# Token sums pinned in one head, seven-product units moved apart, and low parts made by ScalarE and an adding DMA in a hybrid decoder layer

## The chip, the cores and the metric

One core of a Trainium2 chip runs one launch of the kernel. The metric is the device time of that launch in microseconds, the median over several runs. A second figure beside it is the span of one profiled execution, from the first to the last instruction.

## The reference

The layer has 256 tokens, a model width of 2048 and one input matrix that feeds two token mixers side by side. Cut to what matters here:

```python
h = rmsnorm(x, pre_norm_g)
q_a, c_kv, k_rope, z_mla, c_in, b_gate, c_gate, z_conv, g_mla, g_conv = split(h @ w_in)
y_mla  = (causal_mla_attention(q_a, c_kv, k_rope) * silu(z_mla)) @ w_o_mla
y_conv = (b_gate * short_conv(c_gate * c_in) * silu(z_conv)) @ w_o_conv
merged = sigmoid(g_mla) * y_mla + sigmoid(g_conv) * y_conv
return x + rmsnorm(merged @ w_out, post_norm_g)
```

Everything is float32. The change concerns `g_mla` and `g_conv`, two products of the 256 x 2048 normalised input with 2048 x 2048 matrices, which the kernel calls the gate blocks, and some preparation for them during the attention heads.

## The kernel before, in words

**Precision.** TensorE multiplies in a rounded float32 form (`F32R`). Each operand is therefore split into a high part (the rounded value) and a low part (the rest). A product a*b is three matmuls: high*high, high*low, low*high (`product`, L252). The split of a weight is `split_act` (L267): ScalarE copies the raw weight into the rounded tile (L268), and VectorE subtracts that from the raw weight (L269).

**Units.** All weights come as a list of units, `plan`, each 128 x 2048 numbers, 1 MB, in the order in which TensorE uses them. SyncE issues a unit's load into one of three `raw` buffers (`load_raw`, L154, the DMA at L161). `split_unit` (L170) makes the parts, in one of three `whi` and one of three `wlo` buffers (`slot`, L166). `take(i)` (L237) is called when TensorE's matmuls of unit i are written down. In the gate blocks it first asks for the splits up to unit i+2 and the loads up to unit i+3 (L239). With three slots, unit i+2 uses the slot of unit i-1, so its split can start when the matmuls of unit i-1 are done, and it has the time of units i and i+1.

**Order.** Matmuls, and whatever goes through `keep_in_program_order`, keep the order of the program on their engine. All other instructions are placed by a planner that runs a timing model when the kernel is built: among instructions of an engine that it takes to be ready, the earlier in the program goes first. On the chip each engine then runs its list strictly in order. The DMAs on GpSimd's queue that turn tiles around (L355, L359) and that bring shifted rows for the short convolution (L753) are pinned; so are the convolution's additions on VectorE (L769).

**Heads.** Sixteen heads, `for h in range(H)`, each with four units of one channel product (`channels(h, 0..3)`, tiles `cv`), and between them the scores (`sc`), the softmax, the turning of the probabilities (`pt`) and the values (`o`). In odd heads up to 13 one more unit, ahead of the last channel unit, makes the next heads' queries and keys (`qn`, `kn`). After the heads come four gate blocks (matrix n, half b), then the products `sq` with `w_o_mla` and `w_o_conv`, then `out`.

**Gate blocks.** `gate_block` (L936) works on 1024 output columns and has eight units. Five are plain ("whole"): two 128-row slices of the weight, four outputs (two token tiles by two column halves), so 2 x 4 products or 24 matmuls. Three are pairs: two slices k and k+4 that are combined as in Strassen's scheme (Winograd's form), seven products in place of eight, so 21 matmuls. For a pair, `split_pair` (L204) first forms sums and differences of the four raw quarters on VectorE (`tf` and one quarter of `raw`, three instructions at L212), then splits `raw` into `whi`, `wlo` and `tf` into `thi`, `tlo`. There is one `tf`, one `thi` and one `tlo` buffer. The other side of the pairs is the same for all blocks: `token_sums` (L782) forms sums of token tiles (`xf`, L790 to L795) and splits them into `xs`; VectorE does all of it but four copies by ScalarE. It is called once, in head 13, ahead of that head's last channel unit, and its instructions are not pinned.

After the last pair of a block (L968) the products 1, 5, 6 and 7 are joined: ScalarE copies products 1 and 5 from PSUM (L971, L972), VectorE forms `u` in three instructions (L974 to L976). At the block's end VectorE adds these to the four outputs (L980) and ScalarE takes the sigmoid (L981).

The order of a block's units is made by `gate_kinds` (L1105): pair, plain, pair, plain, pair, plain, plain, plain; in the first block the last two plain ones stand in front.

Of the kernel before, what the change touches and what calls it, by code (L numbers as in the profile page):

```python
# [12 lines left out]
F32R = mybir.dt.float32r  # L13
I32 = mybir.dt.int32
AF = mybir.ActivationFunctionType
ALU = mybir.AluOpType
PSUM = bass.MemoryType.PSUM

P = 128
# [3 lines left out]
KD = D // P  # L23
H = 16
# [60 lines left out]
def tile_layer(ctx: ExitStack, tc: tile.TileContext, xw, x, pos, pvec, post_g, wc, wz, wcv, wkr, wqk, wqr, wv, cwr, wsq, wg, out):  # L85
# [84 lines left out]
    def split_unit(i):  # L170
        t, (_, w, kind) = raws.pop(i), plan[i]
        if i == u_kr:
            t = t[:, :w].rearrange("p (k c) -> p k c", k=KD)
            both, parts = slot(i, False)[0], []
            for h in range(2):
                part = both[:, h * HALF : (h + 1) * HALF].rearrange("p (k j c) -> p k j c", k=KD // 2, j=2)
                split_act(part[:, :, 0], part[:, :, 1], t[:, h * KD // 2 : (h + 1) * KD // 2])
                parts.append(part.rearrange("p k j c -> p k (j c)"))
            splits[i] = parts
            return  # L180
        if i <= u_qa[-1]:

            hi, lo = slot(i)
            for j in range(2):
                k, o = 2 * i + j, j * XW
                src = x_first if k == 0 else t[:, o : o + S]
                split_scaled(x_both, src, k)
                split_act(hi[:, j * R : (j + 1) * R], lo[:, j * R : (j + 1) * R], t[:, o + S : o + XW], True)
            splits[i] = hi, lo
            return  # L190
        if u_out[3, 0] <= i < u_out[3, 3]:
            hi, lo = (op.tile([P, UNIT], F32R, name=f"w{o}{i}") for o in ("hi", "lo"))
        else:
            hi, lo = slot(i)
        if kind == "pair":
            splits[i] = split_pair(i, t, hi, lo)
            return
        n = HALF if kind == "half" else UNIT
        for h in range(0, w, n):
            e = min(h + n, w)  # L200
            split_act(hi[:, h:e], lo[:, h:e], t[:, h:e])
        splits[i] = hi, lo
# [64 lines left out]
    def split_act(hi, lo, src, keep=False):  # L267
        a = nc.scalar.activation(hi, src, AF.Copy)  # L268
        b = nc.vector.tensor_tensor(lo, src, hi.bitcast(F32), op=ALU.subtract)  # L269
        if keep:  # L270

            tc.keep_in_program_order(a)
            tc.keep_in_program_order(b)
# [508 lines left out]
    def token_sums(pool):  # L782


        both = x_both[:, :, :].bitcast(F32).rearrange("p (g k) c -> p g k c", k=STEP)[:, :2, :PAIRS]
        xs = pool.tile([P, 4, PAIRS, 2, P], F32R, name="xs")
        xf = pool.tile([P, 2, PAIRS, S], F32, name="xf", tag="tf", bufs=1)
        tt = nc.vector.tensor_tensor
        for g in range(2):
            tt(xf[:, g], both[:, g, :, :S], both[:, g, :, S:], op=ALU.add)  # L790
        (a11, a21), (a12, a22) = [[xf[:, g, :, t * P : (t + 1) * P] for t in range(NT)] for g in range(2)]
        tt(a22, a21, a22, op=ALU.add)
        tt(a21, a11, a21, op=ALU.subtract)
        tt(a11, a22, a11, op=ALU.subtract)
        tt(a12, a12, a11, op=ALU.subtract)  # L795
        for i, f in enumerate((a22, a11, a21, a12)):
            split_act(xs[:, i, :, 0], xs[:, i, :, 1], f)
        return xs

    cv_w = bp.tile([P, NT, 512], F32, name="cv_w")  # L800
    tap, coming, ps_by_head = None, [], {}
# [7 lines left out]

    dstack = main.enter_context(ExitStack())  # L810

    for h in range(H):
        v, at = divmod(h, HV)

# [35 lines left out]
        else:  # L850
            pt = turn(ps_by_head.pop(h - 1))
        channels(h, 1)
        if at == 0:
            arrive()
            coming.append(gates_turn(v, 1))
        else:
            values(h - 1, pt)
# [7 lines left out]
        if at and h < H - 1:  # L865
            arrive()
        channels(h, 2)
        if at == 0:
            arrive()
            if v:  # L870
                coming.append(channels_join(v - 1, 0))
# [6 lines left out]
        if h == H - 3:  # L878
            lstack.close()
            d0 = dstack.enter_context(tc.tile_pool(name="d0", bufs=1))  # L880
            xs = token_sums(d0)
        channels(h, 3)
        if at == 0:
            while coming:
                arrive()
# [45 lines left out]
    def wide(name):  # L931
        return d1.tile([P, 512], F32, name=name, tag=name, bufs=1)
# [3 lines left out]
    def gate_block(n, b, last):  # L936
# [6 lines left out]
        for i, (kind, _) in enumerate(kinds):  # L943
            for m in TAGS if kind == "pair" else ():
                ends[m] = i
            for m in (2, 3, 4, 0) if kind == "whole" else ():
                ends[m] = i
        last_pair = max(i for i, (kind, _) in enumerate(kinds) if kind == "pair")

# [4 lines left out]
        for i, (kind, ks) in enumerate(kinds):  # L954
            if last:
                for v in {6: (0, 1), 7: (2,)}.get(i, ()):
                    split_branch(v)
            w = take(units[i])
            if kind == "pair":
                for m in TAGS:  # L960
                    if m:
                        add_to(m, side(m, ks[0]), w[m], i, True)
            else:
                for m, t, half in ((2, 0, 0), (3, 0, 1), (4, 1, 0), (0, 1, 1)):
                    for j, k in enumerate(ks):
                        a = [x_both[:, k, o + t * P : o + (t + 1) * P] for o in (0, S)]
                        add_to(m, a, w(2 * j + half, 512), i, j == len(ks) - 1)
            if i == last_pair:  # L968
                p1, p5 = wide("p1"), wide("p5")
                u = d1.tile([P, 3, 512], F32, name="u", tag="u", bufs=1)  # L970
                nc.scalar.activation(p1[:, :], ps[1][:, :], AF.Copy)  # L971
                nc.scalar.activation(p5[:, :], ps[5][:, :], AF.Copy)  # L972
                tt = nc.vector.tensor_tensor
                tt(u[:, 0], ps[6][:, :], p1[:, :], op=ALU.add)  # L974
                tt(u[:, 2], ps[7][:, :], u[:, 0], op=ALU.add)
                tt(u[:, :2], u[:, 0::2], p5[:, :].rearrange("p (o c) -> p o c", o=1).to_broadcast([P, 2, 512]), op=ALU.subtract)  # L976
        for m, t, half, other in ((2, 0, 0, p1[:, :]), (3, 0, 1, u[:, 0]), (4, 1, 0, u[:, 2]), (0, 1, 1, u[:, 1])):
            o = 1024 * b + 512 * half
            g = sg[:, n, t, o : o + 512]
# [125 lines left out]
def gate_kinds():  # L1105

    pairs = [("pair", (k, k + STEP)) for k in range(PAIRS)]
    paired = {k for _, ks in pairs for k in ks}
    rest = [k for k in range(KD) if k not in paired]
    plain = [("whole", ks) for ks in zip(rest[::2], rest[1::2])]  # L1110
    alternate = []
    for i, pair in enumerate(pairs):
        alternate += [pair, plain[i]]
    alternate += plain[PAIRS:]
    late = plain[-2:] + [u for u in alternate if u not in plain[-2:]]
    return {(n, b): late if n == b == 0 else alternate for n in range(2) for b in range(2)}


def _cols(w):
# [99 lines left out]
```

## Time and profile before

| | |
|---|---|
| median of 3 runs | 1051.96 us (1051.76 to 1052.58) |
| the profiled execution, its own time | 1052.53 us |
| its span | 1050.7 us |
| TensorE matmul busy | 1026.5 us, 98% |
| VectorE busy | 743.0 us, 71% |
| ScalarE busy | 532.5 us, 51% |
| GpSimd busy | 180.7 us, 17% |
| mean granted TensorE clock | 0.991 |
| DMA | 231.00 MB, mean 220 GB/s |

The profile's page gives each engine's busy time, the chain of work that ended last, and groups of instructions with the idle time in front of them and what ended it. A row `PE sc L90 <- DVE kn L269: 5.8, 1, 5.8` of the waits reads: TensorE's matmuls into `sc`, issued at line 90, waited for VectorE's instruction on `kn` at line 269, 5.8 us in total, once, 5.8 us the longest. A row of the timeline has start, length, engine, line, operation, output and inputs with their shapes, the count, and in brackets the idle time of the engine before it and what ended that. A row of the windows table has, for a stretch of time, the busy time of TensorE, its weight loads, VectorE, ScalarE and GpSimd, each with the number of instructions, then the granted TensorE clock, the DMA engines' busy share and GB/s.

### The profile page before, as it was taken

What the parts mean: (1) busy time and instruction counts of PE and PEld (TensorE: products, weight loads), DVE (VectorE), ACT (ScalarE), POOL (GpSimd) and SP (SyncE); (2) the same over time, 40 slices, a digit from 0 to 9 for tenths busy, and PEclk for the clock granted to TensorE, in tenths of its full rate; (3) what the DMA queues carried; (4) which work ended last, traced back from release to release, by engine and by line L of the source; (5) the groups of instructions that cost most, each with busy time, mean ns of one, the idle gap of its engine ahead of it and who ended that gap; (6) DMA issues with size and microseconds to landing.
All of it is one profiled execution on the core that took longest, in us unless ns stands there. A gap on an engine that the chain in (4) does not pass through costs nothing.

```text
span 1050.7 us, 12467 instructions
## 1 busy us (share of the span) xinstructions
PE 1026.5 (98%) x4658; PEld 852.6 (81%) x4658; DVE 743.0 (71%) x960; ACT 532.5 (51%) x675; POOL 180.7 (17%) x345
## 2 busy tenths in 40 slices
PE   9999999999999999999998999899999999999997
PEld 7887888888888888888886878688888888888885
DVE  7578759677687767777776799788885545666562
ACT  7766546455555455564553545555564433333451
POOL 7621220204212142112312220000000000232000
PEclk9999999999999999999998999899999999999998
DMA  8754765668666685765765765455555555677842
GB/s 337 295 199 177 257 212 212 226 214 275 197 243 195 226 284 199 244 216 203 264 231 196 248 216 186 165 194 202 200 206 195 199 200 192 220 252 247 330 160 80
DMA packets 41948, 231.00 MB, mean 220 GB/s; under 512 B 7520, under 2 KB 8224, under 8 KB 18976
## 3 DMA queue, kind: packets, MB, share of 16 engines
q1 hardware_dynamic: 29808, 197.54, 52.8%
q0 software_dynamic: 11648, 29.38, 9.1%
q10 hardware_dynamic: 432, 3.29, 0.8%
q8 instruction: 36, 0.59, 0.2%
q14 instruction: 24, 0.20, 0.0%
HBM read 214.48 MB, written 11.53 MB: 215 GB/s over the span
## 4 chain that ended last, share of the span: by engine, by line
PE 83%; DVE 9%; issue 4%; ACT 2%; DMA 1%; SPq 0%; DVEq 0%; ACTq 0%
PE cv L90 28%; PE sq L90 17%; PE g L90 10%; PE z L90 8%; PE out L90 8%; DVE wlo L269 4%; PE qn L90 2%; PE ckv L90 2%; ACT whi L268 2%; PE kn L90 2%; PE qa L90 2%; PE vv L90 2%; PE sc L90 1%; PE o L90 1%; DVE tlo L269 1%
## 5 line engine op out<-in xcount | busy, mean ns | idle before, releaser
L269 DVE TENSOR_TENSOR wlo<-raw,whi 128x1024 fp32r<-128x1024 f32 (+2 forms) x290 | 423.5, 1485 | 229.0 <-ACT whi L268 228.4
L268 ACT ACTIVATE whi<-raw 128x1024 fp32r<-128x1024 f32 (+2 forms) x292 | 357.3, 1259 | 373.8 <-PE sq L90 96.9
L90 PE MATMUL cv<-whi,x_both 128*128 128x512 f32 x1024 | 324.1, 391 | 2.7 <-DVE cv_w L736 2.7
L90 PEld LDWEIGHTS cv<-whi,x_both 128*128 128x128 f32 x1024 | 192.9, 188 | 43.1 <-DVE cv_w L736 3.7
L90 PE MATMUL cv<-wlo,x_both 128*128 128x512 f32 x512 | 200.2, 391 | 0.0
L90 PE MATMUL g<-whi,x_both 128*128 128x512 f32 x368 | 119.8, 390 | 0.0
L90 PEld LDWEIGHTS cv<-wlo,x_both 128*128 128x128 f32 x512 | 96.4, 188 | 18.8
L90 PEld LDWEIGHTS g<-whi,x_both 128*128 128x128 f32 x368 | 69.5, 189 | 14.6
L90 PE MATMUL z<-whi,x_both 128*128 128x512 f32 x256 | 80.6, 390 | 0.0
L90 PE MATMUL sq<-whi,x_both 128*128 128x512 f32 x256 | 79.0, 389 | 0.0
L90 PE MATMUL sq<-whi,cv_both 128*128 128x512 f32 x256 | 79.0, 389 | 0.0
L90 PE MATMUL out<-whi,x_both 128*128 128x512 f32 x256 | 79.0, 389 | 0.0
L355 POOL DMA_DIRECT2D far<-via x64 | 35.3, 559 | 225.8 <-DVE via L348 224.8
L90 PE MATMUL g<-wlo,x_both 128*128 128x512 f32 x184 | 71.8, 390 | 0.0
L355 POOL DMA_DIRECT2D far<-sg x32 | 17.5, 552 | 311.5 <-DVE sg L1025 270.2
L90 PEld LDWEIGHTS sq<-whi,x_both 128*128 128x128 f32 x256 | 48.0, 188 | 10.0
L90 PEld LDWEIGHTS sq<-whi,cv_both 128*128 128x128 f32 x256 | 48.0, 188 | 9.9
L90 PEld LDWEIGHTS out<-whi,x_both 128*128 128x128 f32 x256 | 48.0, 188 | 9.9
L90 PEld LDWEIGHTS z<-whi,x_both 128*128 128x128 f32 x256 | 48.1, 188 | 9.9
L90 PE MATMUL z<-wlo,x_both 128*128 128x512 f32 x128 | 49.8, 389 | 0.0
L90 PE MATMUL sq<-wlo,x_both 128*128 128x512 f32 x128 | 49.8, 389 | 0.0
L90 PE MATMUL sq<-wlo,cv_both 128*128 128x512 f32 x128 | 49.8, 389 | 0.0
(242 smaller groups left out, 1327.6 us busy)
## 6 DMA issues: line engine op xcount, KB each, us to landing
raw<-wcv_dram SPq DMA_DIRECT2D x64, 1024.0 KB, 5.4
raw<-wsq_dram SPq DMA_DIRECT2D x48, 1024.0 KB, 4.8
raw<-wg_dram SPq DMA_DIRECT2D x32, 1024.0 KB, 4.7
raw<-wz_dram SPq DMA_DIRECT2D x16, 1024.0 KB, 4.8
raw<-wqk_dram SPq DMA_DIRECT2D x8, 1024.0 KB, 6.7
cw<-cwr_dram POOLq DMA_DIRECT2D x24, 256.0 KB, 6.3
raw<-wc_dram SPq DMA_DIRECT2D x4, 1024.0 KB, 10.0
raw<-wv_dram SPq DMA_DIRECT2D x4, 1024.0 KB, 5.3
```

The source lines that it names most:

```text
L90: return tc.keep_in_program_order(nc.tensor.matmul(*a, **kw))
L268: a = nc.scalar.activation(hi, src, AF.Copy)
L269: b = nc.vector.tensor_tensor(lo, src, hi.bitcast(F32), op=ALU.subtract)
L355: tc.keep_in_program_order(nc.gpsimd.dma_start(out=f[i], in_=m))
```

## The change

**Token sums.** `token_sums` becomes a generator. Its tiles are still made in head 13; its instructions are now pinned on VectorE and (the four copies) ScalarE, and stand in head 14 in three places: the two additions of high and low parts after channel unit 1, four sums and differences after unit 2, the four splits after unit 3.

**Order of the units.** The pairs stand at places 0, 3 and 5 of a block (1, 3 and 5 in the first), so two other units lie between the first and the second, one between the second and the third, and two between the third and the next block's first.

**Added units.** The plain units at places 2 and 6 of each block, eight in all, are of a new kind. ScalarE writes the negative rounded weight into `wlo`; a DMA on GpSimd's queue adds the raw weight to it, read once more from DRAM; ScalarE then makes `whi`. VectorE has no part in it. These DMAs are not pinned. They are 1 MB each.

**Joining.** Product 5 is no longer copied by ScalarE; the last step of `u` is two VectorE instructions that read it in PSUM, in place of one.

```diff
--- before.py
+++ after.py
@@ -194,6 +194,12 @@
             hi, lo = slot(i)
         if kind == "pair":
             splits[i] = split_pair(i, t, hi, lo)
+            return
+        if kind == "added":
+            nc.scalar.activation(lo[:, :], t[:, :], AF.Copy, scale=-1.0)
+            nc.gpsimd.dma_start(out=lo[:, :], in_=plan[i][0].bitcast(F32R), accum_op=ALU.add)
+            nc.scalar.activation(hi[:, :], t[:, :], AF.Copy)
+            splits[i] = hi, lo
             return
         n = HALF if kind == "half" else UNIT
         for h in range(0, w, n):
@@ -785,17 +791,25 @@
         both = x_both[:, :, :].bitcast(F32).rearrange("p (g k) c -> p g k c", k=STEP)[:, :2, :PAIRS]
         xs = pool.tile([P, 4, PAIRS, 2, P], F32R, name="xs")
         xf = pool.tile([P, 2, PAIRS, S], F32, name="xf", tag="tf", bufs=1)
-        tt = nc.vector.tensor_tensor
+
+        def tt(*a, op):
+            tc.keep_in_program_order(nc.vector.tensor_tensor(*a, op=op))
+
+        yield xs
         for g in range(2):
             tt(xf[:, g], both[:, g, :, :S], both[:, g, :, S:], op=ALU.add)
+            yield
         (a11, a21), (a12, a22) = [[xf[:, g, :, t * P : (t + 1) * P] for t in range(NT)] for g in range(2)]
         tt(a22, a21, a22, op=ALU.add)
         tt(a21, a11, a21, op=ALU.subtract)
+        yield
         tt(a11, a22, a11, op=ALU.subtract)
         tt(a12, a12, a11, op=ALU.subtract)
+        yield
         for i, f in enumerate((a22, a11, a21, a12)):
-            split_act(xs[:, i, :, 0], xs[:, i, :, 1], f)
-        return xs
+            split_act(xs[:, i, :, 0], xs[:, i, :, 1], f, True)
+            if i % 2:
+                yield
 
     cv_w = bp.tile([P, NT, 512], F32, name="cv_w")
     tap, coming, ps_by_head = None, [], {}
@@ -809,6 +823,7 @@
 
     dstack = main.enter_context(ExitStack())
 
+    sums = None
     for h in range(H):
         v, at = divmod(h, HV)
 
@@ -850,6 +865,9 @@
         else:
             pt = turn(ps_by_head.pop(h - 1))
         channels(h, 1)
+        if h == H - 2:
+            next(sums)
+            next(sums)
         if at == 0:
             arrive()
             coming.append(gates_turn(v, 1))
@@ -865,6 +883,9 @@
         if at and h < H - 1:
             arrive()
         channels(h, 2)
+        if h == H - 2:
+            next(sums)
+            next(sums)
         if at == 0:
             arrive()
             if v:
@@ -878,8 +899,12 @@
         if h == H - 3:
             lstack.close()
             d0 = dstack.enter_context(tc.tile_pool(name="d0", bufs=1))
-            xs = token_sums(d0)
+            sums = token_sums(d0)
+            xs = next(sums)
         channels(h, 3)
+        if h == H - 2:
+            next(sums)
+            next(sums)
         if at == 0:
             while coming:
                 arrive()
@@ -943,7 +968,7 @@
         for i, (kind, _) in enumerate(kinds):
             for m in TAGS if kind == "pair" else ():
                 ends[m] = i
-            for m in (2, 3, 4, 0) if kind == "whole" else ():
+            for m in (2, 3, 4, 0) if kind != "pair" else ():
                 ends[m] = i
         last_pair = max(i for i, (kind, _) in enumerate(kinds) if kind == "pair")
 
@@ -966,14 +991,14 @@
                         a = [x_both[:, k, o + t * P : o + (t + 1) * P] for o in (0, S)]
                         add_to(m, a, w(2 * j + half, 512), i, j == len(ks) - 1)
             if i == last_pair:
-                p1, p5 = wide("p1"), wide("p5")
+                p1 = wide("p1")
                 u = d1.tile([P, 3, 512], F32, name="u", tag="u", bufs=1)
                 nc.scalar.activation(p1[:, :], ps[1][:, :], AF.Copy)
-                nc.scalar.activation(p5[:, :], ps[5][:, :], AF.Copy)
                 tt = nc.vector.tensor_tensor
                 tt(u[:, 0], ps[6][:, :], p1[:, :], op=ALU.add)
                 tt(u[:, 2], ps[7][:, :], u[:, 0], op=ALU.add)
-                tt(u[:, :2], u[:, 0::2], p5[:, :].rearrange("p (o c) -> p o c", o=1).to_broadcast([P, 2, 512]), op=ALU.subtract)
+                for o in (1, 0):
+                    tt(u[:, o], u[:, 2 * o], ps[5][:, :], op=ALU.subtract)
         for m, t, half, other in ((2, 0, 0, p1[:, :]), (3, 0, 1, u[:, 0]), (4, 1, 0, u[:, 2]), (0, 1, 1, u[:, 1])):
             o = 1024 * b + 512 * half
             g = sg[:, n, t, o : o + 512]
@@ -1107,13 +1132,15 @@
     pairs = [("pair", (k, k + STEP)) for k in range(PAIRS)]
     paired = {k for _, ks in pairs for k in ks}
     rest = [k for k in range(KD) if k not in paired]
-    plain = [("whole", ks) for ks in zip(rest[::2], rest[1::2])]
-    alternate = []
-    for i, pair in enumerate(pairs):
-        alternate += [pair, plain[i]]
-    alternate += plain[PAIRS:]
-    late = plain[-2:] + [u for u in alternate if u not in plain[-2:]]
-    return {(n, b): late if n == b == 0 else alternate for n in range(2) for b in range(2)}
+    plain = list(zip(rest[::2], rest[1::2]))
+    kinds = {}
+    for block in range(4):
+        at = (0, 3, 5) if block else (1, 3, 5)
+        left, units = iter(plain), []
+        for i in range(KD // 2):
+            units.append(pairs[at.index(i)] if i in at else ("added" if i in (2, 6) else "whole", next(left)))
+        kinds[divmod(block, 2)] = units
+    return kinds
 
 
 def _cols(w):
```

## Prediction

> **What bounds the kernel now.** I read the page first, then TensorE's waits, then a table of windows over the heads and gate blocks, then the timeline there.
>
> ```profile
> span 1050.7 us, 12467 instructions
> PE 1026.5 (98%) x4658; PEld 852.6 (81%) x4658; DVE 743.0 (71%) x960; ACT 532.5 (51%) x675; POOL 180.7 (17%) x345
> ```
> ```profile
> PE sc L90 <- DVE kn L269: 5.8, 1, 5.8
> PE g L90 <- DVE tlo L269: 4.1, 3, 2.5
> PE cv L90 <- DVE cv_w L736: 2.7, 4, 0.8
> PE sc L90 <- DVE qr L269: 1.7, 1, 1.7
> PE idle L90 <- POOL hpi L292: 1.1, 1, 1.1
> PE g L90 <- ACT thi L268: 1.0, 1, 1.0
> ```
> ```profile
> core 0: us, PE busy (x) PEld busy (x) DVE busy (x) ACT busy (x) POOL busy (x), PEclk, DMA share, GB/s
> 556.00:583.50 27.50, 26.38 (x116) 21.92 (x116) 18.53 (x39) 11.53 (x21) 6.38 (x13) 0.91 0.52 163
> 606.50:650.00 43.50, 42.39 (x188) 34.76 (x187) 39.83 (x37) 22.16 (x16) 5.49 (x10) 1.00 0.60 211
> 650.00:692.00 42.00, 38.51 (x157) 31.05 (x156) 32.83 (x25) 20.95 (x16) 0.00 (x0) 0.92 0.50 180
> ```
>
> TensorE is idle for 1050.7 - 1026.5 = 24.2 us. The six waits make 16.4 us of it; the rest, 7.8 us, lies behind the last matmul. So nothing is to be had but waits, and what they leave behind: after the 5.8 us wait the granted clock of the next 27.5 us is 0.91 (27.5 x 0.09 = 2.5 us lost), and after the waits in the second gate block it is 0.92 over 42 us (3.4 us).
>
> The change touches two places. At the first head after 13, matmuls `sc` wait 5.8 us for `kn`, which VectorE splits too late. In the gate blocks, `g` waits 4.1 + 1.0 us for the parts of pairs. With the clock this is 5.8 + 2.5 + 4.1 + 1.0 + 3.4 = 16.8 us, the most that the change can plainly win.
>
> **The token sums.** VectorE at the end of head 13:
>
> ```profile
> 545.59 1.83 DVE L790 TENSOR_TENSOR xf<-x_both 128x768 f32<-128x768 f32 x2 [0.47 <-PE kn L90]
> 550.07 0.56 DVE L792 TENSOR_TENSOR xf<-xf 128x384 f32<-128x384 f32 x1
> 556.19 0.76 DVE L269 TENSOR_TENSOR kn<-f,kn 128x256 fp32r<-128x256 f32 x2
> ...
> 566.41 2.36 DVE L269 TENSOR_TENSOR wlo<-raw,whi 128x1024 fp32r<-128x1024 f32 x2 [3.29 <-ACT whi L268]
> 571.90 2.36 DVE L269 TENSOR_TENSOR wlo<-raw,whi 128x1024 fp32r<-128x1024 f32 x2 [3.13 <-ACT whi L268]
> ```
>
> The sums are two additions (1.83 us), four sums or differences and four splits at 0.56 us: 1.83 + 8 x 0.56 = 6.3 us. They stand between the end of `kn`'s matmuls and `kn`'s split. Without them the split lies some 5 to 6 us earlier, about where TensorE comes to it. The same place in head 5, which has no sums, shows no wait:
>
> ```profile
> 274.42 5.47 PE cv L90 x24
> 279.88 0.94 PE sc L90 x8
> ```
>
> 274.42 + 5.47 = 279.89, and `sc` starts at 279.88. So I take the whole 5.8 us and the 2.5 us of clock.
>
> What is late next is head 14. There the sums go in front of VectorE's later pinned work, the convolution's additions and the tiles and transfers on GpSimd's queue behind these; those results are wanted only after the gate blocks, so they can bear some us. The idle time in front of the two splits above is 3.29 + 3.13 = 6.4 us, and the sums are 6.3 us: they just fit. The four copies on ScalarE come last and are wanted only by the first pair. If the sums fit badly, `cv_w` is read late and TensorE waits for its PSUM bank; that wait is there in four heads already, 2.7 us in all. Its cost lies between 0 and 6.3 us. I take 1.0, nearer to zero, because VectorE is busy for 18.53 of that window's 27.5 us and can take the 6.3 in 9.0.
>
> **The gate blocks: VectorE.** One pair and one plain unit of the second block, what a block's end adds, and TensorE's pace:
>
> ```profile
> 642.41 0.69 DVE L974 TENSOR_TENSOR u<-g,p 128x512 f32<-128x512 f32 x1 [0.34 <-PE g L90]
> 646.30 1.22 DVE L976 TENSOR_TENSOR u<-u,p 128x1024 f32<-128x1024 f32 x1
> 649.11 0.68 DVE L980 TENSOR_TENSOR sg<-g,p 128x512 f32<-128x512 f32 x1
> 649.71 2.28 DVE L269 TENSOR_TENSOR wlo<-raw,whi 128x2048 fp32r<-128x2048 f32 x1
> 651.91 1.88 DVE L980 TENSOR_TENSOR sg<-g,u 128x512 f32<-128x512 f32 x3
> 653.70 1.22 DVE L212 TENSOR_TENSOR tf<-raw 128x1024 f32<-128x1024 f32 x1
> ...
> 657.77 4.49 DVE L269 TENSOR_TENSOR wlo<-raw,whi 128x2048 fp32r<-128x2048 f32 x2 [1.39 <-ACT whi L268]
> 662.18 1.75 DVE L269 TENSOR_TENSOR tlo<-tf,thi 128x1536 fp32r<-128x1536 f32 x1
> ```
> ```profile
> 719.22 62.63 PE g L90 x275
> ```
>
> A pair and a plain unit take VectorE from 653.70 to 663.93, 10.2 us, of which the plain one is 2.3 and the pair 7.9 (1.39 of it waiting for ScalarE). TensorE needs 62.63 / 275 = 0.228 us a matmul, so 21 x 0.228 = 4.8 for a pair and 5.5 for a plain unit, 10.25 together. Where pair and plain alternate, VectorE has no slack at all, and the end of a block (two of the 0.69 us kind, L974 and L975, which have one shape, then 1.22, 0.68 and 1.88: 5.2 us) pushes it behind. That is the lateness of `tlo`.
>
> A block: before, 3 x 7.9 + 5 x 2.3 + 5.2 = 40.4 us of VectorE against (63 + 120) x 0.228 = 41.7 us of TensorE. After, two plain units leave VectorE (-4.6) and the last step of `u` is two instructions of 0.69 in place of one of 1.22 (+0.2): 36.0 against 41.7. Between the first two pairs lie 10.9 us of TensorE in which VectorE has one plain unit, and the end of a block meets two other units before the next pair. So the waits for `tlo` and `thi` should go, 5.1 us and 3.4 of clock. Two pairs with one unit between remain (places 3 and 5), as everywhere before, but now VectorE comes to them without a backlog. In the first block the first pair is one place earlier; VectorE has idle time shortly ahead of it:
>
> ```profile
> 596.74 2.29 DVE L269 TENSOR_TENSOR wlo<-raw,whi 128x2048 fp32r<-128x2048 f32 x1 [3.89 <-ACT whi L268]
> ```
>
> The 3.89 us hold the pair's sums (in the rows above 657.77 - 653.70 - 1.39 = 2.7 us). So I cost the earlier place at nothing; without that cover it would cost those 2.7 us once.
>
> **The adding DMA.** This is new, with no row for it. The chain of an added unit runs: slot free, ScalarE writes the negative (1.92 us), GpSimd issues, the DMA lands, TensorE's second matmul of the unit.
>
> ```profile
> 677.11 1.92 ACT L268 ACTIVATE whi<-raw 128x2048 fp32r<-128x2048 f32 x1 [3.49 <-PE g L90]
> 649.88 0.72 ACT L981 ACTIVATE sg<-sg,r_both 128x512 f32<-128x512 f32 x1 [2.63 <-issue]
> 652.63 1.95 ACT L981 ACTIVATE sg<-sg,r_both 128x512 f32<-128x512 f32 x3 [2.03 <-DVE sg L980]
> ```
> ```profile
> 606.50:782.00 175.50, 170.45 (x737) 139.64 (x736) 149.71 (x123) 94.30 (x74) 5.49 (x10) 0.98 0.56 198
> ```
> ```profile
> raw<-wg_dram SPq DMA_DIRECT2D x28, 1024.0 KB, 4.7
> ...
> cw<-cwr_dram POOLq DMA_DIRECT2D x1, 256.0 KB, 3.8
> ```
>
> The time there is: one pair and one plain unit, 10.25, and the first matmul, 0.23, so 10.5 us from the free slot. Less 1.92 for ScalarE and 0.2 for two hand-overs, 8.4 us are left to the DMA if ScalarE starts at once. At place 6 it nearly does: 8. At place 2 the slot comes free at the block's border, where ScalarE's list holds the sigmoids; in the row above they kept it from 649.88 to 654.58. With VectorE in time, one of them (0.72 and its addition) stands ahead: 8.4 - 1.5 = 6.9; at worst 8.4 - 4.7 = 3.7. The second copy to `whi` queues behind the negative on ScalarE, 1.92 us more, and has 6 us to spare.
>
> The DMA's own time: at 198 GB/s and 0.56 of the engines' time, 1.05 MB occupies the engines for 1.05 / 0.198 x 0.56 = 3.0 us, and a load lands after 4.7. From GpSimd, 0.26 MB (0.74 us of moving) landed after 3.8, so 3.1 us go beside the moving. One pass over the megabyte: 3.1 + 3.0 = 6.1 us. If the sum reads its destination in a pass of its own, 9.1. A load beside it adds up to 3.0, so the ends are 6.1 and 12.1. I take 7.5, one pass and half a load beside it (0.56 of the engines' time is taken), because the nearest row, the plain load, moves the same bytes. The Trainium skill ("DMA: Bandwidth & Descriptors", the measured table for GpSimd's queue) gives 6.15 us of moving for 1 MB, which would be about 9 us here with the 3.1 as an estimate from both, and 2 us late at place 2; the trace's 3.0 us of moving for SyncE's loads speaks against so much.
>
> Late at place 2 by 7.5 - 6.9 = 0.6 us, four times: 2.4 us. At place 6: none.
>
> **Sum.** 1052.5 (the profiled execution) - 16.8 + 1.0 + 2.4 = 1039.1. The median of the runs lies 0.6 below that execution: 1038.5.
>
> **Rivals.**
>
> *The adding DMA is late.* At 9.1 us it is 2.2 us late at place 2 and 1.1 at place 6: 4 x 3.3 = 13.2 us of waits. A wait of 2.5 us stood ahead of the 3.4 us of slow clock, so add four of those: 26.8. From 1052.0 - 16.8 + 1.0 = 1036.2 that makes 1063. At 12.1 us each of the eight waits for 4 to 5 us: 8 x (4.7 + 3.4) = 65, 1101. It decides from 16 / 8 = 2 us of lateness in the mean, less if the clock drops. For it: an addition must read what it adds to, and the loads fill 0.56 of the engines. Against: the nearest row gives 6.1 us, and at that every added unit is in time. The Trainium skill ("DMA: Bandwidth & Descriptors", rules for kernel authors) says that an accumulating DMA reads its destination and writes it later; no run here shows yet what that costs. Chance 0.27: slower 0.20, about as before (2 us late) 0.06, a little faster 0.01.
>
> *The sums only move their wait.* Head 14 pays all 6.3 us at `cv_w`, and the clock drops there: 1038.5 + 5.3 + 2.5 = 1046. For it: VectorE's list is in order, and the sums are pinned ahead of later work. Against: the idle 6.4 us. Chance 0.09.
>
> *The added units do not get their early start.* The DMA of the first block's place 2 stands on GpSimd's queue behind the turning of the last channel tiles:
>
> ```profile
> 615.54 2.17 POOL L355 DMA_DIRECT2D far<-mv  x4 [0.26 <-DVE mv L348]
> ```
> ```profile
> 606.65 0.39 PE L90 MATMUL g<-whi,x_both 128*128 128x512 f32 x1
> ```
>
> Issued at 617.7 it lands at 625.2; TensorE, whose gate blocks start at 606.65, wants it at 606.65 + 10.5 = 617.1. One wait of 8 us and 2.5 of clock: 1049. For it: that queue is in order, and these are earlier in the program. Against: the planner sees their inputs as late too. Chance 0.06.
>
> **The numbers.** My forecast has 0.58, with 1034 to 1045 as its own range. A measurement of this kernel can tell about 0.2%, 2.1 us, from no change. Faster: 0.58 + 0.09 + 0.06 + 0.01 = 0.74; the same 0.06; slower 0.20. The low end, 1034, is all 16.8 us with a little of the `cv_w` waits; the high end takes in a DMA of 9.1 us, 1063, and leaves the rest of that rival, some 0.15, outside.
>
> **What would show it.** Right: no wait of `sc` for `kn` and none of `g` for `tlo`; granted clock 1.00 in both windows; VectorE near 36 us in a block; adding DMAs landing in 7 to 8 us, with waits of `g` for them only at place 2. Wrong: eight waits of `g` for `wlo` of 2 us or more and a granted clock near 0.9 across all four blocks; or a wait for `cv_w` of several us at the end of head 14.

## The result and the profile after

| | before | after |
|---|---|---|
| median of 4 runs each, same chip | 1052.27 us (1051.76 to 1053.13) | 1071.24 us (1070.44 to 1072.01) |
| ratio | | 1.0179, 95% interval 1.0162 to 1.0197 |
| profiled execution, span | 1052.53, 1050.7 us | 1071.35, 1069.6 us |

The kernel became 19 us slower, where 13.5 us less was forecast. The page of the kernel after, a line of its head and a row of its DMA part (size and median us from issue to landing at the end):

```profile
PE 1031.3 (96%) x4658; PEld 854.6 (80%) x4658; DVE 726.6 (68%) x956; ACT 544.6 (51%) x679; POOL 188.3 (18%) x353
```
```profile
wlo<-wg_dram POOLq DMA_DIRECT2D x8, 1024.0 KB, 9.7
```

VectorE has 743.0 - 726.6 = 16.4 us less to do, as meant. TensorE's waits after:

```profile
PE g L90 <- DMA wlo<-wg_dram: 10.7, 5, 4.5
PE g L90 <- DVE tlo L275: 7.9, 4, 2.3
PE g L90 <- ACT thi L274: 6.1, 1, 6.1
PE cv L90 <- DVE cv_w L742: 2.7, 4, 0.8
```

The 5.8 us of `sc` for `kn` are gone and `cv_w` is where it was. In the gate blocks 24.7 us of waits stand against 5.1 before: 10.7 for the adding DMAs, but also 14.0 for `tlo` and `thi`, the two waits that were to vanish. The windows after (head 14, then the first and the third of four windows over the gate blocks; the other two are at a clock of 1.00):

```profile
556.00:583.50 27.50, 27.07 (x125) 22.26 (x124) 24.35 (x48) 16.55 (x28) 6.24 (x12) 1.00 0.67 221
606.50:660.00 53.50, 41.71 (x153) 32.96 (x154) 31.47 (x26) 26.23 (x17) 7.34 (x12) 0.84 0.69 216
708.00:756.00 48.00, 43.79 (x183) 35.32 (x183) 31.71 (x28) 26.36 (x19) 1.71 (x2) 0.96 0.70 219
```

The granted clock of head 14 went from 0.91 to 1.00. In the gate blocks it lost 0.16 x 53.5 + 0.04 x 48 = 10.5 us against 3.4 before. The account: +19.6 (waits of `g`) - 5.8 (`sc`) - 2.5 (clock of head 14) + 7.1 (clock of the gate blocks) = +18.4; the two profiled executions differ by 18.8. TensorE's busy time, for the same 4658 matmuls, grew by 1031.3 - 1026.5 = 4.8 us, which agrees with the two clock terms (7.1 - 2.5).

**Why `thi` and `tlo` come late.** TensorE's first matmul of the gate blocks, then VectorE, ScalarE and GpSimd ahead of and at the first pair, after the change (four answers of the timeline):

```profile
598.94 0.39 PE L90 MATMUL g<-whi,x_both 128*128 128x512 f32 x1
```
```profile
589.02 2.29 DVE L275 TENSOR_TENSOR wlo<-raw,whi 128x2048 fp32r<-128x2048 f32 x1 [3.54 <-ACT whi L274]
...
599.47 0.69 DVE L775 TENSOR_TENSOR cv_f<-cv_f,cw 128x512 f32<-128x512 f32 x1 [2.87 <-DMA cw<-cwr_dram]
...
602.81 1.18 DVE L218 TENSOR_TENSOR tf<-raw 128x1024 f32<-128x1024 f32 x1
```
```profile
605.56 1.91 ACT L274 ACTIVATE whi<-raw 128x2048 fp32r<-128x2048 f32 x1 [6.04 <-DVE raw L218]
607.38 1.89 ACT L201 ACTIVATE whi<-raw 128x2048 fp32r<-128x2048 f32 x1
609.18 1.47 ACT L274 ACTIVATE thi<-tf 128x1536 fp32r<-128x1536 f32 x1
610.55 1.89 ACT L199 ACTIVATE wlo<-raw 128x2048 fp32r<-128x2048 f32 x1
```
```profile
612.75 0.95 POOL L200 DMA_DIRECT2D wlo<-wg_dram  x1 [1.27 <-ACT wlo L199]
```

The pair's sums (L218) are pinned on VectorE. In its list they stand behind the convolution's pinned instructions (L775), of which one, a product with the convolution's weights `cw`, stands still until the transfer of these weights lands at 599.4; the first sum comes only at 602.81, behind that product and four more instructions. Measured from the start of the gate blocks (598.94, before 606.65) the pair is wanted one unit of 5.5 us earlier than before, and the convolution is no earlier with that: its transfer was issued at 594.27, 4.7 us ahead of the blocks, and before at 601.07, 5.6 us ahead. In the kernel before, the first of the pair's sums even stood ahead of the product that needs that transfer, and the second behind it:

```profile
605.00 1.22 DVE L212 TENSOR_TENSOR tf<-raw 128x1024 f32<-128x1024 f32 x1
...
606.80 0.68 DVE L769 TENSOR_TENSOR cv_f<-cv_f,cw 128x512 f32<-128x512 f32 x1
...
608.05 0.69 DVE L212 TENSOR_TENSOR raw<-raw,tf 128x512 f32<-128x512 f32 x1
```

Sums and convolution alternate there, although both are pinned, so a pin does not hold these two groups in the one common order that the description of the kernel gives. What puts all the sums behind in the kernel after is not shown; that they stand ahead without the pin is (below).

The idle time that the prediction counted on is still there: 3.54 us ahead of the row at 589.02, and another 2.87 at 599.47. But both lie ahead of the sums in VectorE's list, and what stands behind cannot use them. ScalarE then stands still for 6.04 us behind those sums. After the pair's `whi` its list has the second copy of the added unit of place 2 (L201, 1.89 us), which is wanted later; only then come `thi`, at 609.18, and the negative of that unit, with which its own chain begins. That unit's DMA is issued at 612.75, when TensorE, had it not waited for `thi`, would have come to the unit 3.5 us earlier (598.94 + 5.5 + 4.8 = 609.2).

At the start of a later block (the second) the lists differ, and the effect is the same. ScalarE, then VectorE:

```profile
656.36 1.92 ACT L274 ACTIVATE whi<-raw 128x2048 fp32r<-128x2048 f32 x1 [3.39 <-PE g L90]
658.18 1.47 ACT L274 ACTIVATE thi<-tf 128x1536 fp32r<-128x1536 f32 x1
```
```profile
659.64 2.28 DVE L275 TENSOR_TENSOR wlo<-raw,whi 128x2048 fp32r<-128x2048 f32 x1
...
662.44 1.75 DVE L275 TENSOR_TENSOR tlo<-tf,thi 128x1536 fp32r<-128x1536 f32 x1
```

The planner put the `whi` of the next plain unit (place 1) ahead of the `thi` of the pair at place 0. That `whi` needs a slot that TensorE frees only at 656.3, so ScalarE idles for 3.39 us with `thi` behind it; VectorE then makes the plain unit's `wlo` and one sum of the block's end before `tlo`, which TensorE has been waiting for.

### The profile page after: what moved, and what is told of

The parts are those of the page before. It is cut to its first block, busy times and chain, and to the rows that moved or that the text cites. A ratio compares the mean times of both kernels' runs of the same rounds, so it can differ in the third digit from the quotient of the medians.

```text
span 1069.6 us, 12483 instructions
## 1 busy us (share of the span) xinstructions
PE 1031.3 (96%) x4658; PEld 854.6 (80%) x4658; DVE 726.6 (68%) x956; ACT 544.6 (51%) x679; POOL 188.3 (18%) x353
## 5 line engine op out<-in xcount | busy, mean ns | idle before, releaser
L275 DVE TENSOR_TENSOR wlo<-raw,whi 128x1024 fp32r<-128x1024 f32 (+2 forms) x282 | 405.6, 1462 | 244.7 <-ACT whi L274 242.4
L274 ACT ACTIVATE whi<-raw 128x1024 fp32r<-128x1024 f32 (+2 forms) x284 | 342.2, 1240 | 377.4 <-issue 101.4
L90 PE MATMUL g<-whi,x_both 128*128 128x512 f32 x368 | 123.0, 400 | 0.0
L90 PE MATMUL g<-wlo,x_both 128*128 128x512 f32 x184 | 74.6, 405 | 10.7 <-DMA wlo<-wg_dram 10.7
L90 PEld LDWEIGHTS g<-whi,x_both 128*128 128x128 f32 x368 | 71.8, 195 | 15.2
L90 PEld LDWEIGHTS g<-wlo,x_both 128*128 128x128 f32 x184 | 35.7, 194 | 20.4 <-DMA wlo<-wg_dram 12.8
```

The lines of the kernel that those rows point to most:

```text
L90: return tc.keep_in_program_order(nc.tensor.matmul(*a, **kw))
```

## The experiments

The theories. *O*: the order of the units, by the lists that the planner makes for it, brings the late parts of pairs all by itself. *D*: the adding DMAs make the loss, by landing late and by slowing the loads beside them. For the token sums, *A*: they leave the path and nothing takes their place. In the text of the order alone, D is still called L (late landing); from the repaired lists on, L is theory O (lists), with its rivals named in each text. Every kernel was compared with the kernel before on the same chip, whose medians were 1052.3 to 1052.9 us; a difference between kernels of two sets carries these 0.6 us. The two kernels with a plain copy leave out the subtraction in their added units.

| kernel | us | ratio to before, interval |
|---|---|---|
| token sums alone | 1045.39 | 0.9917 to 0.9950 |
| the change without added units | 1061.62 | 1.0067 to 1.0112 |
| the change, a plain copy for the adding DMA | 1063.35 | 1.0084 to 1.0114 |
| the change, first block in the order of before | 1055.58 | 1.0021 to 1.0054 |
| no added units, later blocks' splits pinned | 1050.67 | 0.9967 to 0.9987 |
| no added units, first block's sums not pinned | 1050.53 | 0.9966 to 0.9988 |
| no added units, both | 1039.96 | 0.9858 to 0.9891 |
| both, and the added units | 1060.56 | 1.0053 to 1.0090 |
| both, and a plain copy for the adding DMA | 1036.53 | 0.9837 to 0.9867 |
| both, and half of each added unit by DMA | 1037.19 | 0.9837 to 0.9870 |
| token sums alone, later blocks' splits pinned | 1041.93 | 0.9884 to 0.9914 |

**The token sums alone** (before, with the new `token_sums` and its calls in head 14).

> The kernel before with the pinned token sums in head 14 and nothing else of the change. Theory A (the sums leave the path and fit into head 14's idle time): the 5.8 us wait of sc for kn and the slow clock after it go, no new wait over 1 us in heads 14 and 15, 1044 to 1045 us. Rival (the sums only move their wait): cv_w is read 3 to 6 us late in head 14, 1049 to 1052 us.

1045.39 us, 6.9 less, 0.4 above the range expected. TensorE's waits:

```profile
PE g L90 <- DVE tlo L275: 4.1, 3, 2.5
PE cv L90 <- DVE cv_w L742: 2.8, 4, 0.9
...
PE g L90 <- ACT thi L274: 1.2, 1, 1.2
```

The wait for `kn` is gone, `cv_w` has 2.8 us for 2.7, and the gate blocks are as before. Theory A holds.

**The order alone** (the change without added units):

```diff
-            units.append(pairs[at.index(i)] if i in at else ("added" if i in (2, 6) else "whole", next(left)))
+            units.append(pairs[at.index(i)] if i in at else ("whole", next(left)))
```

> The changed kernel with the added units split by ScalarE and VectorE like the other plain ones; sums, order of the units and joining stay as changed. Theory L (late landing: the adding DMAs and the loads that they slow down make all the waits of the gate blocks): no waits of g over 1 us are left, 1036 to 1040 us. Theory O (lists: a good part of the waits, 6.1 us for thi in the first block and 2.3 us for tlo at the start of each later block, comes from the order of the instructions on ScalarE and VectorE that goes with the new order of the units): these waits stay, some 17 us with the clock, and only the 16 us of the waits for wlo and their clock go, 1053 to 1057 us.

1061.62 us (its runs lie between 1059.65 and 1064.83): 16.2 more than the sums alone, with no added unit in the kernel, and 4.6 above what theory O expected at most.

```profile
PE g L90 <- DVE tlo L275: 11.5, 4, 3.1
PE g L90 <- ACT thi L274: 5.7, 1, 5.7
```

Theory O holds for the larger part of the loss: 17.2 us of waits for the parts of pairs, where the sums alone leave 5.3. Without the added units the time fell by 9.6 us, not by the 16 of their waits and clock, because the waits for `tlo` grew from 7.9 to 11.5. This kernel also has the changed joining. No wait of TensorE is for its tiles, but the joining was never tried by itself.

**A plain copy in place of the adding DMA**:

```diff
-            nc.gpsimd.dma_start(out=lo[:, :], in_=plan[i][0].bitcast(F32R), accum_op=ALU.add)
+            nc.gpsimd.dma_start(out=lo[:, :], in_=plan[i][0].bitcast(F32R))
```

> The changed kernel with a plain copy in place of the adding DMA: the low parts of the eight units are overwritten with the raw weights, so the subtraction is left out there. If the addition costs a pass over the destination, the copies land after 6 to 7 us in place of 9.0 to 10.8, the waits of g for wlo go but for the first block's, and the time is 1058 to 1064 us. If a megabyte issued by GpSimd is slow by itself, they land after 9 to 10 us again and the time stays at 1069 to 1073.

1063.35 us, 7.9 less than the change, inside the first of the two ranges.

```profile
PE g L90 <- DVE tlo L275: 10.3, 4, 3.1
PE g L90 <- ACT thi L274: 5.9, 1, 5.9
...
PE g L90 <- DMA wlo<-wg_dram: 0.3, 1, 0.3
```
```profile
wlo<-wg_dram POOLq DMA_DIRECT2D x8, 1024.0 KB, 7.0
```

The copy lands after 7.0 us instead of 9.7, and its waits go from 10.7 to 0.3 us. What is left is the waits of the order. So it is the addition that is late, not the second megabyte.

**The first block in the order of before** (the change, but with pairs at places 2, 4 and 6 of the first block and no added unit in it):

```diff
+        if block == 0:
+            by_at = lambda *n: [("pair", (k, k + STEP)) if k < PAIRS else ("whole", plain[k - PAIRS]) for k in n]
+            units = by_at(6, 7, 0, 3, 1, 4, 2, 5)
```

> The changed kernel with the first gate block as in the kernel before: two plain units, then pair and plain in turn, no added units; the other three blocks as changed. By the rows of the changed kernel the first block's waits for thi, tlo and wlo with their clock make 21 us, in place of 1.4 before; the other blocks keep 2.6 us for tlo and 1.5 to 1.9 for wlo each, 14 us. If these add up, 1050 to 1053 us. If the first block's waits are only moved into the second, 1058 or more.

1055.58 us, 15.7 less than the change, but 2.6 above the 1053 expected at most: the first block alone holds most of the loss. It is less than all that TensorE loses there, since a new wait has come, for `u`, at the border to the second block; the later blocks keep their waits for `tlo` and for the DMAs of place 6.

```profile
PE g L90 <- DVE tlo L275: 6.4, 3, 2.3
PE g L90 <- DMA wlo<-wg_dram: 4.5, 3, 1.6
...
PE g L90 <- DVE u L1001: 2.1, 1, 2.1
```

**The lists repaired, one half at a time.** All three kernels have the new order and no added units. The first pins the splits of the later blocks (the flag `keep` of `split_act`), so that ScalarE makes the pair's `whi` and `thi` before the next unit's `whi`; the second takes the pin off the sums of the first block's pairs; the third does both. In the kernel with the order alone 9.3 us of waits (three of 3.1) stand in the later blocks and 7.9 in the first; the texts reckon with 13.3 and 10.6.

```diff
-            split_act(hi[:, h:e], lo[:, h:e], t[:, h:e])
+            split_act(hi[:, h:e], lo[:, h:e], t[:, h:e], u_g[1][0] <= i < u_d[0][0][0])
...
-            tc.keep_in_program_order(nc.vector.tensor_tensor(*a, op=op))
+            a = nc.vector.tensor_tensor(*a, op=op)
+            if i >= u_g[1][0]:
+                tc.keep_in_program_order(a)
...
-        split_act(hi[:, :], lo[:, :], t[:, :])
-        split_act(thi[:, :, :], tlo[:, :, :], tf[:, :, :])
+        keep = i >= u_g[1][0]
+        split_act(hi[:, :], lo[:, :], t[:, :], keep)
+        split_act(thi[:, :, :], tlo[:, :, :], tf[:, :, :], keep)
```

> The new order with no added units, and in blocks 1 to 3 the splits of units pinned to the program's order on ScalarE and VectorE, so that ScalarE makes the pair's whi and thi before the next plain unit's whi, and VectorE makes tlo before that unit's wlo. Theory L (the late parts of pairs are a matter of the order of the engines' lists): the waits of blocks 1 to 3, 13.3 us in the kernel with the order alone, nearly go; the first block's 5.9 and 4.8 us stay; 1061.6 - 13.3 = 1048.3, 1046 to 1051. Rival W (VectorE and ScalarE have too much work there, whatever the order): the waits only go to another unit, wlo in place of tlo, and the time stays at 1058 or more.

> The new order with no added units, and in the first block the sums of a pair's quarters not pinned on VectorE, so that they can stand ahead of the convolution's additions, which wait for their rows. Theory L: the first block's waits for thi and tlo, 5.9 and 4.8 us, go; the later blocks' 13.3 us stay; 1061.6 - 10.6 = 1051, 1049 to 1054. Rival R (the first pair is late because its raw tiles and ScalarE's copies come late): the waits stay within 2 us, 1059 to 1062.

> Both edits of the engines' lists, no added units. Theory L: the gate blocks lose 1 to 4 us in all, less than in the kernel before (9.0): 1061.6 - 10.6 - 13.3 = 1037.7, 1036 to 1042, less than the kernel with the token sums alone (1045.4). Rival W or R: 1048 or more.

Pinning: 1050.67 us, 10.9 less (13.3 expected). Its waits of `g`, then those of the kernel with the first block's sums free, 1050.53 us, 11.1 less (10.6 expected):

```profile
PE g L90 <- ACT thi L275: 6.0, 1, 6.0
PE g L90 <- DVE tlo L276: 4.3, 6, 2.2
```
```profile
PE g L90 <- DVE tlo L277: 9.3, 3, 3.1
```

Each edit takes away the waits of its own blocks, but for 2.1 us, and leaves the others: the 6.0 us for `thi` and 2.2 of those for `tlo` stand in the first block, the three of 3.1 us in the later ones. Without the pin, the first pair's sums stand in the very idle time that the prediction counted on, and its weights had landed by then:

```profile
586.51 1.22 DVE L218 TENSOR_TENSOR tf<-raw 128x1024 f32<-128x1024 f32 x1 [0.81 <-DMA raw<-wg_dram]
```

With both, 1039.96 us, 21.7 less; the two gains alone add up to 22.0. The start of the second block in that kernel, on ScalarE and on VectorE:

```profile
652.14 1.92 ACT L277 ACTIVATE whi<-raw 128x2048 fp32r<-128x2048 f32 x1 [4.36 <-DVE raw L218]
653.96 1.47 ACT L277 ACTIVATE thi<-tf 128x1536 fp32r<-128x1536 f32 x1
```
```profile
656.30 1.75 DVE L278 TENSOR_TENSOR tlo<-tf,thi 128x1536 fp32r<-128x1536 f32 x1
657.97 2.28 DVE L278 TENSOR_TENSOR wlo<-raw,whi 128x2048 fp32r<-128x2048 f32 x1
```

These are the instructions that the rows of the kernel after show, with the same durations, but `thi` follows its `whi` at once and `tlo` stands before the plain unit's `wlo`. Of the waits for `tlo` 2.0 us are left, and none for `thi`. Theory L holds, and rivals W and R fall.

**The added units on repaired lists** (both edits, and the added units as in the change).

> Both edits of the engines' lists, and the added units with their adding DMAs at places 2 and 6 again, so the whole change with its lists repaired. Theory D (the adding DMA takes 9 to 11 us and slows the loads beside it, which is later than TensorE wants the unit): waits for wlo of 1.5 us or more at each place 6 and some at place 2, 5 to 12 us above the kernel with both edits and without added units, 1043 to 1050. Rival V (the added units relieve VectorE, and the waits for their DMAs came from late starts in disordered lists): within 2 us of that kernel or below it, 1036 to 1040.

1060.56 us, 20.6 more than without added units, above even what theory D expected. Nothing but the adding DMAs is waited for in the gate blocks now:

```profile
PE g L90 <- DMA wlo<-wg_dram: 15.7, 8, 4.3
```
```profile
756.00:800.00 44.00, 39.70 (x163) 32.24 (x163) 29.44 (x29) 24.84 (x24) 0.86 (x1) 0.92 0.59 195
```

All eight are waited for, and the granted clock drops behind them, to 0.92 in the fourth block's window (the row has the columns of the windows above). Its GpSimd queue from 600 to 785 us (packets, MB, share of the 16 engines) and the landing of the loads beside it:

```profile
q0 software_dynamic: 1568, 9.44, 25.8%
...
raw<-wg_dram SPq DMA_DIRECT2D x27, 1024.0 KB, 7.5
```

For the additions, the view of their line of the code gives the shortest, the median and the longest:

```profile
DMA to landing us min/median/max: 9.2/9.3/11.8
```

The four waits at place 2 are under 1 us, where 9.2 to 9.5 us lie between the issue and the end of the wait; of those at place 6 three are 3.5 to 4.3 us, where it is 11.3 to 11.9. Rival V falls: late starts weren't the cause.

**A plain copy on repaired lists** (as above, without the addition).

> Both edits of the engines' lists, and the added units with a DMA that copies the raw weight into wlo in place of adding it (so the subtraction of the rounded weight is left out of these units); all else as with the adding DMAs, 1060.6 us. Theory D (it is the addition that is late): the copy lands after 7 us in place of 9.3 and the loads beside it after 5 in place of 7.2, the eight waits for wlo go or stay under 1 us, 1040 to 1046. Rival T (the second megabyte of a unit and ScalarE's second copy cost this, whatever the DMA does): 1054 or more.

1036.53 us, below even what theory D gave, and no wait of `g` at all; TensorE's only waits left are the 3.1, 1.7 and 1.1 us of `cv_w`, `qr` and the end. The same view:

```profile
q0 software_dynamic: 1569, 9.44, 14.5%
...
raw<-wg_dram SPq DMA_DIRECT2D x27, 1024.0 KB, 6.4
wlo<-wg_dram POOLq DMA_DIRECT2D x8, 1024.0 KB, 5.9
```

The same 9.44 MB on GpSimd's queue take 14.5% of the engines' time in place of 25.8%. The view of the kernel with both edits and no added units:

```profile
q0 software_dynamic: 416, 1.05, 1.8%
...
raw<-wg_dram SPq DMA_DIRECT2D x27, 1024.0 KB, 4.8
```

So eight additions take (25.8 - 1.8)% of 185 us, 5.6 us of all 16 engines for one, and a plain copy (14.5 - 1.8)%, 2.9 us. The addition costs the engines nearly twice the time of a copy, and the loads beside it land later too. Theory D holds, rival T falls. But the loads beside a plain copy land later as well, after 6.4 us where the text expected 5; here no matmul waits for it.

**Half of an added unit by DMA** (the same, with one half of the low part made by the adding DMA and the other by VectorE):

```diff
-            nc.scalar.activation(lo[:, :], t[:, :], AF.Copy, scale=-1.0)
-            nc.gpsimd.dma_start(out=lo[:, :], in_=plan[i][0].bitcast(F32R), accum_op=ALU.add)
-            nc.scalar.activation(hi[:, :], t[:, :], AF.Copy)
+            a, b = slice(0, HALF), slice(HALF, UNIT)
+            nc.scalar.activation(lo[:, b], t[:, b], AF.Copy, scale=-1.0)
+            nc.gpsimd.dma_start(out=lo[:, b], in_=plan[i][0][:, b].bitcast(F32R), accum_op=ALU.add)
+            split_act(hi[:, a], lo[:, a], t[:, a])
+            nc.scalar.activation(hi[:, b], t[:, b], AF.Copy)
```

> Both edits of the engines' lists, and added units in which the adding DMA makes only one half of the low part (512 KB); ScalarE and VectorE make the other half as in plain units. Theory D with a landing that goes with the bytes: 512 KB land after 5 to 6.5 us, in time at place 2 and nearly so at place 6, 1039 to 1045. Rival F (most of the landing is there whatever the size, or the addition blocks the loads all the same): landing 8 us or more, waits for wlo of over 6 us in all, 1048 or more.

1037.19 us, the fastest kernel that leaves nothing out: 15.6 us less than before (1052.83) on the same chip, and 2.8 less than without added units. It is below the range of theory D, though the additions land after 6.7 us (the longest after 10.5), a little later than expected. Rival F falls. One of eight is waited for:

```profile
wlo<-wg_dram POOLq DMA_DIRECT2D x8, 512.0 KB, 6.7
```
```profile
PE g L90 <- DMA wlo<-wg_dram: 0.9, 1, 0.9
```

**The order of before with the later blocks' splits pinned** (the sums alone, and the first and the third hunk of the edit of the lists).

> The kernel with the token sums alone (pair and plain unit in turn, no added units, product 5 copied by ScalarE; 1045.4 us), and from the second block on the splits pinned to the program's order on ScalarE and VectorE. Theory L (waits for the parts of pairs come from the order of the lists, and the order of the units has little part in it): waits for tlo fall below 2 us in all, 1039 to 1042, as with the new order and the same pinning (1040.0). Rival B (the balance: where pair and plain alternate VectorE has no slack): 3 us or more of waits stay, 1043.5 to 1047, and the new order is worth the difference.

1041.93 us, 3.5 less than the sums alone, inside what theory L gave for the time; but 3.2 us of `tlo` waits stay where it expected less than 2:

```profile
PE g L90 <- DVE tlo L276: 3.2, 2, 1.8
```

One of the two stands in the first block (1.4 us, at 622 us), which this edit doesn't touch, the other at the second block's first pair. Against the 1039.96 us of the new order with both edits the order of the units is worth some 2.0 us at most, and the first block's edit and the changed joining, which only that kernel has, may be part of it. So this run doesn't decide between L and B for that remainder.

## Why the prediction was wrong

- **Token sums: right.** 8.3 us were to be won and 1.0 lost at `cv_w`, net 7.3; alone they brought 6.9. The wait and the slow clock went, and the rival in which the sums only move their wait didn't happen. But the 1.0 wasn't lost either (2.8 us of waits for 2.7), so the net figure agrees better than its terms, which is partly luck.
- **"So the waits for `tlo` and `thi` should go": this step failed.** It compared 36.0 us of VectorE's work in a block (40.4 before) with TensorE's 41.7 and took the slack for time at hand. The waits didn't come from too much work. For each pair those sums count 1.39 us in which VectorE waits for ScalarE, and in the kernel before the last two blocks, pair and plain in turn as in the others, ran with 0.45 us of waits and with none (the second row reaches past the end of the blocks):

```profile
692.00:734.00 42.00, 41.55 (x184) 34.09 (x183) 35.53 (x28) 23.24 (x17) 0.00 (x0) 1.00 0.56 201
734.00:782.00 48.00, 48.00 (x214) 39.74 (x213) 41.52 (x36) 27.96 (x26) 0.00 (x0) 1.00 0.57 199
```

What makes the waits is the order of the lists. The prediction's own lines already have it for the second block: at 657.77 VectorE makes two `wlo`, the pair's and the next unit's, and only at 662.18 the `tlo` for which TensorE waited 2.5 us. (On the order of before the pins left 3.2 of 5.3 us of waits, so there this is shown in part only.) An engine works through its list in a fixed order, and the new order of the units made new lists, in which `thi` stands behind another unit's `whi`, that has no slot yet in the later blocks, and `tlo` behind the next unit's `wlo`. The order alone cost 16.2 us, and the two edits of the lists took off 21.7 with the same instructions, though every plain unit was still VectorE's. The prediction's sum without lateness of the DMA, 1036.2, can be reached (1036.5 with a plain copy and repaired lists, where no `g` waits), but it took the repair of the lists, which the prediction didn't have.
- **"So I cost the earlier place at nothing": failed for the same reason.** The cover of 3.89 us was read from a row of idle time, without asking where the pinned sums stand in the list. The cover was real, for without the pin the sums stand in it; with the pin they come 16 us later. In the kernel after, 6.1 us of wait for `thi` stand there, some 1.8 of them for the copy at L201. The prediction's price for lost cover, 2.7 us, was too small as well: it is the sums' length, and what is lost is the time of all that stands ahead of them, a transfer among it.
- **The adding DMA: the chain was right, its duration mis-sized.** 7.5 us were taken, one pass over the data and half a load beside it; 9.0 to 10.8 were measured in the kernel after. The prediction's own figure for a second pass, 9.1, was the better one: two passes of 3.0 us stand against 5.6 us of engine time measured, although no run shows that the engines do make two passes. The nearest row, a plain load, was the wrong one to choose by, because an addition does something that a load doesn't. The Trainium skill ("DMA: Bandwidth & Descriptors", the measured table for GpSimd's queue) gives 6.15 us of moving for 1 MB; with the prediction's 3.1 us that made 9 us for a copy too, and the copies here landed after 5.9 and 7.0.
- **The loads beside it were not in the sum.** With the additions they land after 7.5 us, beside plain copies after 6.4, without added units after 4.8. The additions in turn land later at some places than at others: the waits of 3.5 to 4.3 us stand at place 6, where the prediction saw spare time, and those under 1 us at place 2. That it is the loads beside them which make this difference was not tried.
- **The rivals.** *The adding DMA is late* was priced at 1063 us for a landing of 9.1; with repaired lists it gave 1060.6. The mechanism held, the place of the waits didn't, and the price came close by two errors that nearly cancel: 15.7 us of waits for 13.2, and TensorE busy for 9.1 us more than with plain copies (1029.3 against 1020.2) where 13.6 were put down for the clock. The change's 1071.2 lies beyond it because the lists come on top. *The added units do not get their early start* forecast a landing at 625.2 us in the first block; it was about 623.5, but not by GpSimd's queue: in the row above that DMA waits for ScalarE's negative alone.
- **The sums don't simply add.** The added units cost 9.6 us on the disordered lists and 20.6 on the repaired ones: where TensorE already waits for a pair, the transfer gains the same time. This is read from the rows (waits for the additions of 10.7 us against 15.7) and was not tried by itself.

## What to carry to other kernels

Slack in an engine's total is no slack for an instruction that stands behind another one in an ordered list: before a reordering is priced, read which instruction stands ahead of the wanted one on its engine and what that one waits for. When a new order brings waits, look at the lists first; here two small edits of them took away 21.7 us, more than the order had cost. Price an operation that does more than its nearest row by what it does more, and try it at half the size before it is given up.

## What the runs showed of the hardware

- An adding DMA of 1 MB into a tile in SBUF, issued by GpSimd, landed after a median of 9.3 to 10.0 us beside ordinary loads, a plain copy of the same size after 5.9 to 7.0, and an adding one of 512 KB after 6.7. Per megabyte, the addition took 5.6 us of all 16 DMA engines, the copy 2.9. The Trainium skill ("DMA: Bandwidth & Descriptors", rules for kernel authors) names GpSimd as the issuer for accumulating DMAs; what one costs stands in these runs.
- Loads beside the additions land later: 7.5 us from issue to landing with them, 6.4 beside plain copies, 4.8 without added units.
- The granted clock falls behind waits: 0.84 over the 53.5 us that hold those of 6.1 and 4.5 us, so that 24.7 us of waits in the gate blocks cost 10.5 more.
